# The memory's value projection as three float32r products, its norm's small products moved, in a fused decoder layer on one Trainium2 core

## The chip, the core and the metric

The kernel runs on one core of a Trainium2 chip. The core has a matrix engine (TensorE, PE in the profile, with its weight loads as PEld), three engines for elementwise work (VectorE or DVE, ScalarE or ACT, GpSimd or POOL), and SyncE (SP), from which this kernel issues all its DMA transfers. Each engine works through its own list of instructions in the order in which they were built and waits on semaphores for the others. The metric is the device time of one execution in microseconds (us). The median of three runs before the change is 1672.93 us (1672.88 to 1676.76).

## What is computed

One decoder layer over 1024 positions of width 1024. Its input is normalised by its root mean square, one combined projection gives the columns for stick-breaking attention, for an mLSTM and for the queries of a cross-attention into 256 memory tokens. The three branches are merged by gates, then a gated MLP follows. The change lies in what the memory needs:

```python
def _rmsnorm(x, g):
    xf = x.astype(jnp.float32)
    y = xf * lax.rsqrt(jnp.mean(xf * xf, axis=-1, keepdims=True) + EPS)
    return (y * g.astype(jnp.float32)).astype(x.dtype)

def _memory_cross_attention(q, mem_n, w_kv, g_q, g_k):
    k, v = jnp.split(mem_n @ w_kv, 2, axis=-1)
    qh = _rmsnorm(_split_heads(q, XA_HEADS), g_q)
    kh = _rmsnorm(_split_heads(k, XA_HEADS), g_k)
    vh = _split_heads(v, XA_HEADS)
    ...
h = _rmsnorm(x, g_mix[l])
... = jnp.split(h @ w_in[l], offsets, axis=-1)
y_xa = _memory_cross_attention(xa_q, _rmsnorm(mem, g_mem[l]), w_mem_kv[l], xa_g_q[l], xa_g_k[l])
```

The memory's norm is a factor per token, so the kernel projects `mem * g_mem` first and multiplies by the factor when it reads the sums.

## The kernel before

Everything is float32 in memory. A product is done in one of two ways. With float32 operands it is one call on PE, which the trace shows as two matmul records. With the type float32r, each operand is split into two tensors: hi, a rounded copy made by ACT, and lo, the rest, a subtraction on DVE (`split`, lines 135 to 137; `wsplit` allocates the pair). `mm3` (lines 148 to 151) then sums three products: hi by hi, hi by lo and lo by hi.

The start of the program is what the change touches, in the order in which it is written:

- `mem_load` (twice) loads half of the memory, transposed, into a tile of 128 x 1024 (tag `y`) and multiplies it by its gain on ACT (line 196) into a page `mg[j]`.
- `mem_w` loads one of four blocks of the weights for the keys (`w_kv[0]`) or the values (`w_kv[1]`). `mem_mm` multiplies a block with the memory, float32 by float32: four calls for each block (two halves of the tokens, two rows of 128 channels). The keys go to the banks `ps_z`, the values to `ps_pv`.
- `mem_stats` squares the memory (line 211), adds it up and has two small products with a column of ones (line 218), which give the sum per token.
- `x_page` loads the input in pieces of two channels blocks by 512 positions; `x_stats` squares them (line 274) and adds them on DVE (lines 277, 279); `rstd` takes four small products with ones (line 165) and a power on POOL (line 157); `spread` makes a diagonal of the result (line 177) and multiplies it with ones (line 179), so that the factor of each position stands in a row for all partitions. `x_norm` then multiplies the input by gain and factor (line 287) and splits it into `hh` and `hl` (the tiles `h`), and writes the unsplit form to DRAM (`hn_d`).
- After that follow the projections of the upper half of positions: queries and keys of the first head pair (`chunks`, banks `ps_pj`, two of them in turn), the gates (`gates_if`, line 462), then `nat_chunks` for the values. In between the lower half of the input is loaded (`xp[0]`) and normalised in the same way, and `mem_keys` and `mem_values` read the memory's sums.

A bank `ps_pj` is free again when ACT and DVE have read it: lines 374 to 377 for the queries, 381 to 386 for the keys.

The order on each engine is decided when the program is built: a scheduler goes through the calls above and places them by priority (`tc.high_priority` moves a part ahead by a number of places), and tiles with the same tag share a fixed number of buffers (`BUFS`): two each for `raw`, `whi`, `wlo`, five for `U`, sixteen for `pg`.

Of the kernel before, what the change touches and what calls it, by code (L numbers as in the profile page):

```python
# [18 lines left out]
P = 128  # L19
# [23 lines left out]
def tile_hybrid_layer(ctx: ExitStack, tc: tile.TileContext, xT, memT, vecs, w_t, w_n, w_kv, w_if,  # L43
# [143 lines left out]
    mraw = []  # L187
    mg = [page() for _ in range(2)]

    def mem_load(j):  # L190
        t = T([P, S], "y")
        mraw.append(t)
        nc.sync.dma_start(t.rearrange("p (k m) -> p k m", k=4), memT[4 * j:4 * j + 4].rearrange("k p m -> p k m"))
        for i in range(4):
            c = slice(i * NMEM, (i + 1) * NMEM)
            nc.scalar.activation(mg[j][:, c], t[:, c], AF.Copy, scale=col(C_GMEM + 4 * j + i))

    mtags = itertools.cycle(("raw", "whi", "wlo"))

    def mem_w(which, b):  # L200
        t = T([P, S], next(mtags))
        nc.sync.dma_start(t, w_kv[which, b])
# [5 lines left out]

    def mem_stats():
        for t in mraw:  # L210
            nc.scalar.activation(t, t, AF.Square)
        a = mraw[0]
        nc.vector.tensor_add(a, a, mraw[1])
        for n in (512, 256):
            nc.vector.tensor_add(a[:, :n], a[:, :n], a[:, n:2 * n])
        pc = bank("tr")
# [3 lines left out]

    def mem_mm(pm, w, b):
        for m in range(2):
            for kk in range(2):
                k = 2 * b + kk
                c = slice((k % 4) * NMEM + m * P, (k % 4) * NMEM + (m + 1) * P)
                nc.tensor.matmul(pm[m], mg[k // 4][:, c], w[:, hs(kk)], start=(k == 0), stop=(k == KT - 1))  # L226

    def mem_keys(pm, rm):
# [65 lines left out]
    mem_load(0)  # L294
    wk.append(mem_w(0, 0))
    mem_load(1)
    for b in range(1, 4):
        wk.append(mem_w(0, b))
        if b < 3:
# [6 lines left out]
    for g in range(2):  # L306
# [3 lines left out]
        nc.vector.tensor_sub(wif[:, :, 64 + 32 * g:68 + 32 * g], src, hi.bitcast(F32))  # L310
    mem_mm(pk, wk[0], 0)
    mem_mm(pk, wk[1], 1)
    rm = mem_stats()
    mem_mm(pk, wk[2], 2)
    mem_mm(pk, wk[3], 3)
    for b in range(4):
        wv.append(mem_w(1, b))
    r = rstd(x_stats(xp[1]), HALF)
    mem_mm(pv, wv[0], 0)
    x_norm(1, xp[1], spread(r, 4))  # L320
    for b in range(1, 4):
        mem_mm(pv, wv[b], b)

# [176 lines left out]
    for _ in range(3):  # L500
        next(vals)
    kn = mem_keys(pk, rm)
    mem_values(pv, rm)
# [906 lines left out]
```

## Time and profile before

| | before |
|---|---|
| median of three runs | 1672.93 us |
| the profiled execution | 1674.48 us |
| its span, first to last instruction | 1672.4 us |
| PE busy in the span | 1645.0 us (98%) |
| DVE busy | 1209.2 us (72%) |
| ACT busy | 826.8 us (49%) |
| POOL busy | 52.8 us (3%) |
| DMA, mean over the span | 127 GB/s |
| granted TensorE clock, mean | 1.000 |

The page of the profile gives such totals and the groups of instructions that cost most. For an edit in the first 60 us of 1672, the views that tell more are the timeline of each engine (start, length, engine, line, output from inputs, and in brackets how long the engine was idle before and who ended that), the list of waits, and the chain of work that ended last, here asked for a stretch of time. "x8" at the end of a timeline row says that eight instructions were merged into it.

### The profile page before, as it was taken

To read this page: it belongs to the slowest core of one execution; us is meant where nothing else is said; L and a number is where in the kernel's file an instruction comes from. 1 tells how busy PE (TensorE), PEld (TensorE's weight loads), DVE (VectorE), ACT (ScalarE), POOL (GpSimd) and SP (SyncE) were. 2 spreads that over 40 slices of the span, in tenths; PEclk is the share of its full clock that TensorE was granted. 3 is DMA by queue.
4 is the path that set the end of the run, shared out by engine and by line. 5 is a ranking of instruction groups with operands and counts; after the bars stand their busy time and mean duration, and the time that the engine had idled before them with its cause. 6 is when DMAs were issued, how large, how long until landed. Compare 5 with 4: busy or idle time off the path is not lost.

```text
span 1672.4 us, 21192 instructions
## 1 busy us (share of the span) xinstructions
PE 1645.0 (98%) x7975; PEld 1338.0 (80%) x7975; DVE 1209.2 (72%) x1710; ACT 826.8 (49%) x1249; POOL 52.8 (3%) x95
## 2 busy tenths in 40 slices
PE   8999999999999999999999999999999999999999
PEld 4777777788877888888788888688888888788887
DVE  5648778777765666666557648997778877789864
ACT  4547667645555445556422334565455554543431
POOL 1000000010000001000000000000000000000000
PEclk9999999999999999999999999999999999999999
DMA  8410011234324555433755354222222221486131
GB/s 296 149 64 24 35 39 51 95 116 137 108 104 154 183 183 170 133 127 113 271 181 184 114 189 145 94 90 104 78 77 76 82 87 58 164 327 239 36 138 73
DMA packets 96249, 212.69 MB, mean 127 GB/s; under 512 B 12416, under 2 KB 36224, under 8 KB 96148
## 3 DMA queue, kind: packets, MB, share of 16 engines
q1 hardware_dynamic: 96148, 211.35, 37.1%
q8 instruction: 63, 1.03, 0.3%
q14 instruction: 38, 0.31, 0.1%
HBM read 156.71 MB, written 54.61 MB: 126 GB/s over the span
## 4 chain that ended last, share of the span: by engine, by line
PE 89%; DVE 4%; ACT 4%; DMA 3%; issue 1%; SPq 0%; POOLq 0%; POOL 0%; ACTq 0%; DVEq 0%
PE ps_pj L149 14%; PE ps_pj L150 14%; PE ps_pj L151 14%; PE ps_pv L150 6%; PE ps_pv L151 6%; PE ps_pv L149 6%; PE ps_tr L151 4%; PE ps_tr L149 4%; PE ps_tr L150 4%; PE ps_z L149 3%; PE ps_z L150 3%; PE ps_z L151 3%; PE ps_tr L434 2%; PE ps_pv L448 1%; PE ps_z L226 1%; PE ps_z L413 1%
## 5 line engine op out<-in xcount | busy, mean ns | idle before, releaser
L150 PE MATMUL ps_pj<-h,whi 128*128 128x512 f32 x620 | 242.2, 391 | 0.0
L136 ACT ACTIVATE whi<-raw 128x512 fp32r<-128x512 f32 (+1 forms) x112 | 93.6, 836 | 177.5 <-PE ps_pj L150 71.6
L149 PE MATMUL ps_pj<-h,whi 128*128 128x512 f32 x412 | 163.2, 396 | 0.9 <-DVE U L1053 0.9
L149 PE MATMUL ps_pj<-pg,whi 128*128 128x512 f32 x396 | 154.6, 390 | 0.0
L151 PE MATMUL ps_pj<-pg,wlo 128*128 128x512 f32 x380 | 148.0, 389 | 0.0
L150 PEld LDWEIGHTS ps_pj<-h,whi 128*128 128x128 f32 x620 | 116.5, 188 | 23.5 <-issue 0.2
L151 PE MATMUL ps_pj<-h,wlo 128*128 128x512 f32 x332 | 129.9, 391 | 0.1
L810 DVE SCALAR_TENSOR_TENSOR y<-U,vec,y 128x1023 f32<-128x1023 f32 x88 | 112.5, 1280 | 8.0 <-ACT y L808 8.0
L422 DVE TENSOR_TENSOR_SCAN U<-U 128x512 f32<-128x512 f32 (+3 forms) x96 | 88.6, 965 | 30.7 <-ACT U L415 29.8
L149 PEld LDWEIGHTS ps_pj<-h,whi 128*128 128x128 f32 x412 | 77.4, 188 | 18.3 <-issue 1.5
L137 DVE TENSOR_TENSOR wlo<-raw,whi 128x1024 fp32r<-128x1024 f32 x54 | 66.0, 1222 | 30.9 <-ACT whi L136 30.6
L149 PEld LDWEIGHTS ps_pj<-pg,whi 128*128 128x128 f32 x396 | 74.3, 188 | 15.8 <-DVE pg L1051 0.4
L151 PEld LDWEIGHTS ps_pj<-pg,wlo 128*128 128x128 f32 x380 | 71.3, 188 | 14.9 <-issue 0.2
L136 ACT ACTIVATE whi<-pg 128x512 fp32r<-128x512 f32 (+1 forms) x59 | 43.4, 738 | 72.2 <-PE ps_pv L150 20.7
L150 PE MATMUL ps_pj<-pg,whi 128*128 128x512 f32 x188 | 73.4, 390 | 0.0
L151 PEld LDWEIGHTS ps_pj<-h,wlo 128*128 128x128 f32 x332 | 62.3, 188 | 13.6 <-DVE wlo L137 0.6
L150 PE MATMUL ps_pv<-h,whi 128*128 128x512 f32 x164 | 63.8, 389 | 0.0
L808 ACT ACTIVATE y<-U,vec 128x1024 f32<-128x1024 f32 x44 | 54.6, 1241 | 14.7 <-DVE U L712 14.6
L151 PE MATMUL ps_pj<-h,whi 128*128 128x512 f32 x156 | 60.8, 390 | 0.0
L137 DVE TENSOR_TENSOR wlo<-raw,wlo 128x512 fp32r<-128x512 f32 x58 | 39.9, 688 | 23.0 <-ACT wlo L136 22.7
L151 PE MATMUL ps_tr<-pg,wlo 128*128 128x512 f32 x144 | 56.2, 390 | 0.1
L137 DVE TENSOR_TENSOR whi<-raw,whi 128x512 fp32r<-128x512 f32 x58 | 39.9, 688 | 22.0 <-ACT whi L136 22.0
(438 smaller groups left out, 4306.0 us busy)
## 6 DMA issues: line engine op xcount, KB each, us to landing
raw<-in_w_t_dram SPq DMA_DIRECT2D x29, 512.0 KB
gate_d<-U SPq DMA_DIRECT2D x24, 512.0 KB
U<-gate_d SPq DMA_DIRECT2D x24, 512.0 KB
pg<-in_w_up_dram SPq DMA_DIRECT2D x22, 512.0 KB
act_d<-y SPq DMA_DIRECT2D x22, 512.0 KB
pg<-in_w_t_dram SPq DMA_DIRECT2D x21, 512.0 KB
raw<-in_w_dn_dram SPq DMA_DIRECT2D x18, 512.0 KB
raw<-in_w_o_dram SPq DMA_DIRECT2D x16, 512.0 KB
```

Of the source, the lines that this page charges most:

```text
L136: nc.scalar.activation(hi, src, AF.Copy)
L137: (eng or nc.vector).tensor_sub(lo, src, hi.bitcast(F32))
L149: nc.tensor.matmul(out, lh, rh, start=start, stop=False, skip_group_check=more)
L150: nc.tensor.matmul(out, lh, rl, start=False, stop=False, skip_group_check=more)
L151: nc.tensor.matmul(out, ll, rh, start=False, stop=stop, skip_group_check=more)
L226: nc.tensor.matmul(pm[m], mg[k // 4][:, c], w[:, hs(kk)], start=(k == 0), stop=(k == KT - 1))
L413: nc.tensor.matmul(z[:, a, :w], qs[a][:, ts(rb)], kz[a][:, c], start=False, stop=True)
L422: nc.vector.tensor_tensor_scan(f[:, a, 1:w + 1], f[:, a, 1:w + 1], f[:, a, 1:w + 1], 1.0 if o == 0 else f[:, a, 0:1], op0=ALU.mult, op1=AL ...
L434: nc.tensor.transpose(pt[:, a, ts(j)], g[:, a, ts(j)], ident)
L448: nc.tensor.matmul(pv[64 * a:64 * a + 64, ts(rb % 4)], sbv[s // 2][:, s % 2, (2 * p + a) * 64:(2 * p + a + 1) * 64], wt[:, a, ts(j)], star ...
L808: nc.scalar.activation(out, u, AF.Identity, bias=bias, scale=taps[0])
L810: nc.vector.scalar_tensor_tensor(out[:, :S - s], u[:, s:], taps[s], out[:, :S - s], op0=ALU.mult, op1=ALU.add)
```

## The change

The values are now computed with `mem_mm3`, that is with `mm3` on hi and lo of the memory (`mgr`, split in `mem_load`) and of each block of value weights. The keys stay as they are. The weights of the values are loaded into tiles `U`, `raw`, `raw`, `U` and split from there. The squares of the memory are added up by `mem_squares` into a tile `me` after all of this in the text of the program, and the two small products are called (`mem_rstd`) just before `mem_keys`. The small products of the input's norm (`rstd`) are called between the two halves of the last block of keys, and `spread` between the two halves of the first block of values.

```diff
--- before.py
+++ after.py
@@ -186,6 +186,7 @@
     nc.scalar.activation(warm, nhalf[:, :1], AF.Square)
     mraw = []
     mg = [page() for _ in range(2)]
+    mgr = [[page(dt=F32R) for _ in range(2)] for _ in range(2)]
 
     def mem_load(j):
         t = T([P, S], "y")
@@ -194,11 +195,10 @@
         for i in range(4):
             c = slice(i * NMEM, (i + 1) * NMEM)
             nc.scalar.activation(mg[j][:, c], t[:, c], AF.Copy, scale=col(C_GMEM + 4 * j + i))
-
-    mtags = itertools.cycle(("raw", "whi", "wlo"))
-
-    def mem_w(which, b):
-        t = T([P, S], next(mtags))
+        split(mg[j], *mgr[j])
+
+    def mem_w(which, b, tag):
+        t = T([P, S], tag)
         nc.sync.dma_start(t, w_kv[which, b])
         return t
 
@@ -206,24 +206,36 @@
     nc.vector.tensor_mul(gqk, col(C_GQ), col(C_GK))
     xkv_d = dtile([XAH, P, 2, NMEM], "xkv_d")
 
-    def mem_stats():
+    def mem_squares():
         for t in mraw:
             nc.scalar.activation(t, t, AF.Square)
-        a = mraw[0]
-        nc.vector.tensor_add(a, a, mraw[1])
-        for n in (512, 256):
-            nc.vector.tensor_add(a[:, :n], a[:, :n], a[:, n:2 * n])
+        a, b = mraw
+        out = T([P, HALF], "me")[:, :NMEM]
+        nc.vector.tensor_add(a, a, b)
+        nc.vector.tensor_add(a[:, :HALF], a[:, :HALF], a[:, HALF:])
+        nc.vector.tensor_add(out, a[:, :NMEM], a[:, NMEM:HALF])
+        return out
+
+    def mem_rstd(a):
         pc = bank("tr")
         for t in range(2):
             nc.tensor.matmul(pc[:, t:t + 1], a[:, ts(t)], ones[:, :1], start=True, stop=True)
         return rstd_cols(pc[:, :2], 2, D)
 
-    def mem_mm(pm, w, b):
-        for m in range(2):
+    def mem_mm(pm, w, b, ms=(0, 1)):
+        for m in ms:
             for kk in range(2):
                 k = 2 * b + kk
                 c = slice((k % 4) * NMEM + m * P, (k % 4) * NMEM + (m + 1) * P)
                 nc.tensor.matmul(pm[m], mg[k // 4][:, c], w[:, hs(kk)], start=(k == 0), stop=(k == KT - 1))
+
+    def mem_mm3(pm, w, b, ms=(0, 1)):
+        for m in ms:
+            for kk in range(2):
+                k = 2 * b + kk
+                c = slice((k % 4) * NMEM + m * P, (k % 4) * NMEM + (m + 1) * P)
+                mm3(pm[m], mgr[k // 4][0][:, c], mgr[k // 4][1][:, c], w[0][:, hs(kk)], w[1][:, hs(kk)],
+                    k == 0, k == KT - 1)
 
     def mem_keys(pm, rm):
         kns = []
@@ -292,10 +304,10 @@
     xp = {0: [], 1: []}
     wk, wv = [], []
     mem_load(0)
-    wk.append(mem_w(0, 0))
+    wk.append(mem_w(0, 0, "raw"))
     mem_load(1)
     for b in range(1, 4):
-        wk.append(mem_w(0, b))
+        wk.append(mem_w(0, b, ("raw", "whi", "wlo")[b - 1]))
         if b < 3:
             xp[1] += [x_page(1, i) for i in (2 * b - 2, 2 * b - 1)]
     wraw = T([P, KT, 8], "hf")
@@ -308,18 +320,26 @@
         hi = wif[:, :, 32 * g:32 * g + 4]
         nc.scalar.activation(hi, src, AF.Copy)
         nc.vector.tensor_sub(wif[:, :, 64 + 32 * g:68 + 32 * g], src, hi.bitcast(F32))
-    mem_mm(pk, wk[0], 0)
-    mem_mm(pk, wk[1], 1)
-    rm = mem_stats()
-    mem_mm(pk, wk[2], 2)
-    mem_mm(pk, wk[3], 3)
-    for b in range(4):
-        wv.append(mem_w(1, b))
-    r = rstd(x_stats(xp[1]), HALF)
-    mem_mm(pv, wv[0], 0)
-    x_norm(1, xp[1], spread(r, 4))
-    for b in range(1, 4):
-        mem_mm(pv, wv[b], b)
+    for b in range(3):
+        mem_mm(pk, wk[b], b)
+    wraws = [mem_w(1, 0, "U")]
+    a = x_stats(xp[1])
+    wraws += [mem_w(1, b, ("raw", "raw", "U")[b - 1]) for b in range(1, 4)]
+    mem_mm(pk, wk[3], 3, (0,))
+    r = rstd(a, HALF)
+    mem_mm(pk, wk[3], 3, (1,))
+    wv.append(wsplit(None, raw=wraws[0]))
+    mem_mm3(pv, wv[0], 0, (0,))
+    rows = spread(r, 4)
+    wv.append(wsplit(None, raw=wraws[1]))
+    x_norm(1, xp[1], rows)
+    mem_mm3(pv, wv[0], 0, (1,))
+    mem_mm3(pv, wv[1], 1)
+    for b in range(2, 4):
+        with tc.high_priority(offset=200):
+            wv.append(wsplit(None, raw=wraws[b]))
+        mem_mm3(pv, wv[b], b)
+    squares = mem_squares()
 
     def proj(src, rh, rl, consume, halves=(1, 0), tag="pj"):
         wh, wl = wsplit(src)
@@ -499,6 +519,7 @@
     x_norm(0, xp[0], spread(r, 4))
     for _ in range(3):
         next(vals)
+    rm = mem_rstd(squares)
     kn = mem_keys(pk, rm)
     mem_values(pv, rm)
     for _ in range(4):
```

With the scheduler, this moves instructions on all engines up to the normalisation of the lower half of x; behind that the order of every engine is what it was. Three places matter below. Lines of the changed program are numbered 12 to 21 higher than before. In these rows a tile has its buffer's running number, and names ahead of `<-` are written.

DVE, from the normalisation of the upper half of x to the split of the first projection's weights. Line 287 makes a half page of the normalised x, the next row on an `h` is its lo. `wlo_74` and `wlo_78` are the lo of the weights for queries and keys, `pg_64` that of the first weights for the values of the attention. Before (the row behind the last one shown is `wlo_78`):

```order
L137 TENSOR_TENSOR wlo_74_303<-raw_72_300,whi_73_302 128x1024
L137 TENSOR_TENSOR h_16_111<-U_53_232,h_8_103 128x512
L287 SCALAR_TENSOR_TENSOR U_54_240<-pg_32_143,vec_92,ps_tr_51_222 128x512
L137 TENSOR_TENSOR h_17_112<-U_53_232,h_9_104 128x512
L287 SCALAR_TENSOR_TENSOR U_54_240<-pg_32_143,vec_92,ps_tr_51_222 128x512
L137 TENSOR_TENSOR h_18_113<-U_54_240,h_10_105 128x512
L287 SCALAR_TENSOR_TENSOR U_55_248<-pg_33_145,vec_92,ps_tr_51_222 128x512
L137 TENSOR_TENSOR h_19_114<-U_54_240,h_11_106 128x512
L287 SCALAR_TENSOR_TENSOR U_55_248<-pg_33_145,vec_92,ps_tr_51_222 128x512
L137 TENSOR_TENSOR h_20_115<-U_55_248,h_12_107 128x512
L137 TENSOR_TENSOR pg_64_283<-y_62_280,pg_63_282 128x1024
L137 TENSOR_TENSOR h_21_116<-U_55_248,h_13_108 128x512
```

In the changed program `wlo_84` and `wlo_88` belong to queries and keys. The lo of the last two blocks of the memory's value weights, `wlo_62` and `wlo_64`, stand seven and three rows ahead of the first one shown:

```order
L137 TENSOR_TENSOR h_20_115<-U_58_238,h_12_107 128x512
L299 SCALAR_TENSOR_TENSOR U_59_246<-pg_36_151,vec_92,ps_tr_49_199 128x512
L137 TENSOR_TENSOR h_21_116<-U_58_238,h_13_108 128x512
L299 SCALAR_TENSOR_TENSOR U_59_246<-pg_36_151,vec_92,ps_tr_49_199 128x512
L137 TENSOR_TENSOR h_22_117<-U_59_246,h_14_109 128x512
L299 SCALAR_TENSOR_TENSOR U_60_254<-pg_37_153,vec_92,ps_tr_49_199 128x512
L137 TENSOR_TENSOR h_23_118<-U_59_246,h_15_110 128x512
L299 SCALAR_TENSOR_TENSOR U_60_254<-pg_37_153,vec_92,ps_tr_49_199 128x512
L137 TENSOR_TENSOR h_24_119<-U_60_254,h_16_111 128x512
L137 TENSOR_TENSOR wlo_84_353<-raw_82_350,whi_83_352 128x1024
L137 TENSOR_TENSOR h_25_120<-U_60_254,h_17_112 128x512
L137 TENSOR_TENSOR wlo_88_388<-raw_86_385,whi_87_387 128x1024
```

The lo of the weights for the queries has moved from the first third of these rows to their end, with that for the keys two rows behind it, and two splits of the memory's weights stand ahead.

SP, at the loads of the lower half of x (`in_xT_dram`), before:

```order
L142 DMA raw_76_335<-in_w_t_dram 128x1024
L142 DMA raw_85_399<-in_w_n_dram 128x1024
L289 DMA hn_d_117<-U_54_240 128x1024
L289 DMA hn_d_117<-U_55_248 128x1024
L266 DMA pg_68_292<-in_xT_dram 128x2x512
L266 DMA pg_69_294<-in_xT_dram 128x2x512
```

and in the changed program:

```order
L301 DMA hn_d_121<-U_59_246 128x1024
L301 DMA hn_d_121<-U_60_254 128x1024
L142 DMA raw_95_449<-in_w_n_dram 128x1024
L142 DMA raw_98_455<-in_w_n_dram 128x1024
L278 DMA pg_78_342<-in_xT_dram 128x2x512
L278 DMA pg_79_344<-in_xT_dram 128x2x512
```

Two loads of weights now stand ahead of those of x. `raw_98` takes the buffer of `raw_86`, which is free once `wlo_88` has been computed on DVE.

ACT, between the square of the first loaded page of x (`pg_68` before, `pg_78` now) and the last read of the bank of the first keys, before:

```order
L274 ACTIVATE U_93_438<-pg_68_292 128x1024
L374 ACTIVATE pg_56_272<-ps_pj_75_306 64x512
L375 ACTIVATE pg_57_273<-ps_pj_75_306 64x512
L274 ACTIVATE U_94_440<-pg_69_294 128x1024
L274 ACTIVATE U_95_443<-pg_70_296 128x1024
L381 ACTIVATE pg_58_274<-ps_pj_79_341 64x512
L382 ACTIVATE pg_59_275<-ps_pj_79_341 64x512
L383 ACTIVATE pg_58_274<-ps_pj_79_341 64x512
L384 ACTIVATE pg_59_275<-ps_pj_79_341 64x512
```

and in the changed program:

```order
L286 ACTIVATE U_103_488<-pg_78_342 128x1024
L136 ACTIVATE whi_96_451<-raw_95_449 128x1024
L394 ACTIVATE pg_66_322<-ps_pj_85_356 64x512
L395 ACTIVATE pg_67_323<-ps_pj_85_356 64x512
L286 ACTIVATE U_104_490<-pg_79_344 128x1024
L286 ACTIVATE U_105_493<-pg_80_346 128x1024
L286 ACTIVATE U_106_496<-pg_81_348 128x1024
L136 ACTIVATE whi_99_457<-raw_98_455 128x1024
L401 ACTIVATE pg_68_324<-ps_pj_89_391 64x512
L402 ACTIVATE pg_69_325<-ps_pj_89_391 64x512
L403 ACTIVATE pg_68_324<-ps_pj_89_391 64x512
L404 ACTIVATE pg_69_325<-ps_pj_89_391 64x512
```

Two copies of weights and one square have come between the page's arrival and the last read of that bank.

## The prediction

> **What bounds the kernel now.** I read the page's totals first, then PE's waits, then the chain of waits in the stretch that the change touches.
>
> ```profile
> span 1672.4 us, 21192 instructions
> PE 1645.0 (98%) x7975; PEld 1338.0 (80%) x7975; DVE 1209.2 (72%) x1710; ACT 826.8 (49%) x1249; POOL 52.8 (3%) x95
> ```
>
> PE is busy for 98% of the span, so time that is taken from PE or added ahead of it tends to reach the end. The list of PE's waits up to 140 us (engine, line, whom it waited for: total, times, longest) has these at its start:
>
> ```profile
> PE ps_z L226 <- ACT pg L196: 6.9, 1, 6.9
> ...
> PE ps_pj L462 <- DVE pg L377: 0.6, 1, 0.6
> ...
> PE ps_pj L149 <- DVE pg L386: 0.5, 1, 0.5
> ```
>
> After its first product at 6.9 us PE waits only twice in the first 60 us, 1.1 us together, both times for a bank that DVE has yet to read (lines 377 and 386). The chain behind the second wait (start, length, what) shows who set it:
>
> ```profile
> 28.22 2.06 DVE U L287 x3
> ...
> 38.35 0.33 SPq L289
> ...
> 38.73 0.44 SPq L266
> ...
> 40.03 8.37 DMA pg<-in_xT_dram
> ...
> 53.58 0.70 DVE pg L386
> ...
> 54.42 0.47 PE ps_pj L149
> ```
>
> From 28.22 us, when the row factor of the upper half of x is ready, DVE works through the normalisation; SP can issue the loads of the lower half of x (line 266) only behind the last `hn_d` store; ACT squares those pages before it reads the banks; and PE gets its bank at 54.42. PE's full work hides this chain up to 0.5 us. So the question is not only what PE saves, but whether this chain grows.
>
> **What PE saves.** Rows of PE's timeline (start, length, line, output from inputs):
>
> ```profile
> 31.45 3.60 PE L226 MATMUL ps_pv<-raw,pg 128*128 128x512 f32 x8
> 34.89 3.60 PE L226 MATMUL ps_pv<-whi,pg 128*128 128x512 f32 x8
> ...
> 45.62 0.39 PE L151 MATMUL ps_pj<-h,wlo 128*128 128x512 f32 x1
> ...
> 49.02 0.39 PE L151 MATMUL ps_pj<-h,wlo 128*128 128x512 f32 x1
> 49.96 0.45 PE L462 MATMUL ps_pj<-h,pg 128*100 128x512 f32 x1 [0.55 <-DVE pg L377]
> ...
> 53.50 0.40 PE L463 MATMUL ps_pj<-h,pg 128*100 128x512 f32 x1
> ...
> 62.71 0.94 PE L165 MATMUL ps_tr<-ones,U 128*128 128x1 f32 x8
> 63.51 0.49 PE L149 MATMUL ps_pj<-whi,h 128*128 128x512 f32 x1
> ```
>
> A block of value weights takes 34.89 - 31.45 = 3.44 us, four blocks 13.76. The 15 float32r products from 45.62 to 49.02 take 0.227 each; the 48 that replace the four blocks take 10.9. PE saves **2.9 us**. The two small products of the memory's norm move into the stream of float32r products. There eight records of such products took 63.51 - 62.71 = 0.8 us; theirs are four, **0.4 us**, and they come after the stretch below, where nothing takes them in. Where they stood, among the keys, PE now is done earlier but then waits, so I count no gain for it.
>
> **What ACT and DVE get.** The splits are new work for them: six copies and six subtractions of 128x1024. Rows of both, of POOL and PE:
>
> ```profile
> 5.56 1.70 ACT L196 ACTIVATE pg<-y,vec 128x256 f32<-128x256 f32 x4 [3.33 <-DMA y<-in_memT_dram]
> ...
> 10.13 1.06 ACT L211 ACTIVATE y<-y 128x1024 f32<-128x1024 f32 x1
> ...
> 18.46 0.35 ACT L309 ACTIVATE pg<-hf 128x32 fp32r<-128x32 f32 x2 [0.47 <-DMA hf<-in_w_if_dram]
> ...
> 46.24 1.06 ACT L274 ACTIVATE U<-pg 128x1024 f32<-128x1024 f32 x1 [1.36 <-DMA pg<-in_xT_dram]
> ...
> 48.42 2.01 ACT L274 ACTIVATE U<-pg 128x1024 f32<-128x1024 f32 x2
> ```
>
> ```profile
> 11.22 1.23 DVE L213 TENSOR_TENSOR y<-y,y 128x1024 f32<-128x1024 f32 x1 [7.31 <-ACT y L211]
> 12.48 1.15 DVE L215 TENSOR_TENSOR y<-y 128x512 f32<-128x512 f32 x2
> 13.79 0.91 DVE L305 MEMSET pg<- 128x1024 f32 x1 [0.16 <-issue]
> ...
> 19.29 0.69 DVE L279 TENSOR_TENSOR U<-U 128x512 f32<-128x512 f32 x1
> ...
> 25.11 0.88 DVE L177 TENSOR_SCALAR hf<-ident,sm 128x128 f32<-128x128 f32 x4 [1.13 <-POOL sm L157]
> ...
> 40.74 1.22 DVE L137 TENSOR_TENSOR wlo<-raw,whi 128x1024 fp32r<-128x1024 f32 x1
> ```
>
> ```profile
> 16.78 1.70 POOL L157 TENSOR_TENSOR sm<-sm,nhalf 128x2 f32<-128x2 f32 x1 [13.11 <-DVE sm L155]
> 24.07 1.01 POOL L157 TENSOR_TENSOR sm<-sm,nhalf 128x4 f32<-128x4 f32 x1 [5.59 <-DVE sm L155]
> ...
> 27.16 1.02 PE L179 MATMUL ps_tr<-hf,ones 128*128 128x512 f32 x2
> ```
>
> I follow the new order with these lengths up to the row factor of x.
>
> - On ACT each half of the memory now takes gain, copy and square: 5.56 + 2 x (1.70 + 1.06 + 1.06) = 13.2 us, against 11.2 before.
> - DVE then adds the memory's squares and clears the gate-weight page, in this order: 13.2 + 1.23 + 1.15 + 0.91 = 16.5, with the gaps 16.6. The two copies of line 309 wait for that page, and now stand ahead of the squares of x on ACT: 17.0, then four squares at 1.0 (48.42: two in 2.01): 21.0.
> - DVE: three sums from 19.0 on, 22.7; lo of the first value block 23.9; last sum 24.6; lo of the second block 25.8.
> - PE has then finished the keys (6.9 + 1.7 us of slow start, shown below, + 4 x 3.44 = 22.4) and waits for that first lo. Its small products end at 25.4, the scaling on DVE at 26.0. The power on POOL costs 1.01 or 1.70 us: the first of the program took 1.70, and this one is now the first, so 27.7. Diagonals 28.6; the product by line 179 and its way to DVE took 28.22 - 27.16 = 1.1 plus its weight load: **29.9**, against 28.22.
>
> From there to the end of `wlo_78` (40.74 + 1.22 = 41.96) DVE needed 13.74 us before, for eight rows of line 287, eight lo of h and three of 128x1024. The changed order has as many of each up to `wlo_88` (its three are `wlo_64`, `wlo_84`, `wlo_88`), and must wait some 0.4 us for the copy of the fourth block, whose buffer PE frees late: 29.9 + 13.74 + 0.4 = **44.0 us**. The loads of x now stand on SP behind `raw_98`, which waits for `wlo_88`: first x load at 44.4, against 38.73. What is queued on SP behind it, the weights of the next projection, has slack.
>
> How long the load takes is not settled by the trace. The first page of the memory, with little ahead, is the row below; before, the first x page took 46.24 - 38.73 = 7.5 us, behind two stores.
>
> ```profile
> 1.18 4.29 DMA y<-in_memT_dram
> ```
>
> I take 5.0, nearer to the first, since only loads stand right ahead: 49.4 (48.7 to 51.9). Of the stretches of the start, this one (length, busy time of each engine, clock, DMA share, GB/s) has the transfers nearly back to back:
>
> ```profile
> 12.00:23.00 11.00, 11.00 (x32) 5.17 (x30) 7.11 (x11) 4.58 (x6) 1.70 (x1) 1.00 0.94 368
> ```
>
> [...]
>
> Behind the page, ACT and DVE needed 53.58 + 0.70 - 46.24 = 8.04 us before to the end of the second bank's read. Now one more square and two copies of weights stand between: + 3 x 1.02 = 11.1. PE starts its first product of the attention's values at 49.4 + 11.1 + 0.1 = **60.6** instead of 54.42: +6.2. The saving of 2.9 us is inside this number, since PE arrives early and waits. With the 0.4: **+6.6 us**.
>
> After that, the order of all engines is as before, and each later wait of PE hangs on work that starts from PE's own products, so I take the shift to the end. The mem keys now follow the normalisation of the lower half, and PE has banks of 24 products (5.4 us each) to fill meanwhile; their transposes should not wait.
>
> The profiled execution took 1674.48 us (span 1672.4), 1.55 above the median; 1674.48 + 6.6 = 1681.1 for such an execution, **1679.5** for the median of 1672.93.
>
> **The rivals.** A measurement of this kernel can tell about 0.3% (5.0 us) from no change.
>
> *PE's own path decides (not slower).* If the x pages land before 47.8, the banks come early, and what is left is the wait for `wlo_84`: 44.0 - 1.22 - 0.61 = 42.2; the 44 products left of two banks, 10.0 us, and sixteen of line 462 and 463 at (53.50 - 49.96)/15 = 0.236, 3.8, give 56.0: +1.6, with the 0.4 +2.0, 1674.9. It holds up to +5.0, and needs a load in under 3.4 us; for it speaks that loads may run undisturbed by stores, against it the rows of 4.29 and 7.5. Chance 0.2.
>
> *The saving stays.* If DVE's front part is not on the path, PE keeps 2.9 - 0.4 and perhaps the 1.1 of waits: 1669.5, still within 0.3%. Against it: 5.8 us would have to be missing from DVE's sum. Chance 0.02.
>
> *The pages land as late as before.* 7.5 us after issue: 51.9 + 11.2 = 63.1, +8.7 + 0.4: 1682.0. For it: two loads stand just ahead in the queue, and 7.5 and 8.37 are the only values for these pages at this place. Chance 0.2, with a tail beyond.
>
> *A later wait takes part of it in*, one that does not move with PE: PE's waits after 60 us would have to shrink by 2 us or more; 1675 to 1677.5. Chance 0.06.
>
> *PE's tempo falls in its new pause.* At the start, after 6.9 us of rest, weight loads of line 226 followed each other at twice the later distance:
>
> ```profile
> 8.75 0.33 PEld L226 LDWEIGHTS ps_z<-raw,pg 128*128 128x128 f32 x1 [0.52 <-issue]
> 9.60 0.33 PEld L226 LDWEIGHTS ps_z<-raw,pg 128*128 128x128 f32 x1 [0.52 <-issue]
> 10.37 0.19 PEld L226 LDWEIGHTS ps_z<-raw,pg 128*128 128x128 f32 x1 [0.44 <-issue]
> 10.80 0.19 PEld L226 LDWEIGHTS ps_z<-raw,pg 128*128 128x128 f32 x1 [0.24 <-issue]
> ```
>
> 0.85 against 0.43 us, four times: 1.7 us. The longest of PE's waits after that, in the list for the whole span, is no longer than this:
>
> ```profile
> PE ps_pv L149 <- ACT pg L136: 1.7, 1, 1.7
> ```
>
> If the pause before `wlo_84` (from about 38.6 to 42.2, 3.6 us) did the same, PE would be 1.7 us later at the next bank, for which it then waits 4 us anyway: no change to the forecast, and 1676.6 instead of 1674.9 in the first rival. [...]
>
> **How the numbers follow.** Forecast (+5 to +8 us) 0.52; landing late 0.2; PE's own path 0.2; partly taken in 0.06; saving kept 0.02. Slower by over 0.3%: 0.52 + 0.2 + a third of the 0.06 = 0.74; within: 0.25; faster 0.01. The range leaves out half of the first rival and the tail of late landings: 1675.4 to 1683.0. Its ends are those of the load (4.29 and 7.5 us) widened by about 1 us for the sum on DVE and below to the middle of the first rival.
>
> **What would show it.** Right: on SP the first x load near 44.4; ACT's first square of the lower half at 48.7 to 52; PE waits of 3 to 4 us for a lo by line 137 at the queries' bank and of 3 to 5 us for the subtraction that is line 386 now; `ps_pv` products 0.23 apart. Wrong: the row factor's first use well before 29 us, the x load before 42, no wait of PE above 2 us behind 30 us, or a shift that shrinks behind 60 us.

## The result, and the profile after

The changed kernel takes **1682.97 us** (median of 6 runs, 1681.26 to 1684.04), the kernel before 1673.57 us on the same chip (6 runs, 1672.88 to 1676.76). The ratio is **1.0052, 95% interval 1.0041 to 1.0062**: slower by half a per cent. The profiled execution of the changed kernel took 1681.26 us, the fastest of its six. Its page:

```profile
span 1679.5 us, 21243 instructions
PE 1646.5 (98%) x7991; PEld 1343.3 (80%) x7991; DVE 1217.9 (73%) x1716; ACT 831.6 (50%) x1255; POOL 52.2 (3%) x95
```

The span is 7.1 us longer. PE's busy time is no shorter although 2.9 us of work were taken out; the reason is for the most part the clock, below. The list of PE's waits up to 140 us (engine, tile, line, whom it waited for: total, times, longest) now has, of what is new:

```profile
PE ps_z L230 <- ACT pg L197: 6.4, 1, 6.4
PE ps_pj L151 <- DVE wlo L137: 3.1, 1, 3.1
PE ps_pj L482 <- DVE pg L397: 2.3, 1, 2.3
...
PE ps_pj L149 <- DVE pg L406: 0.8, 1, 0.8
```

The chain that the prediction follows, in rows of the timeline (start, length, engine, line, output from inputs, in brackets the idle time ahead and who ended it):

```profile
25.63 1.03 POOL L157 TENSOR_TENSOR sm<-sm,nhalf 128x4 f32<-128x4 f32 x1 [21.97 <-DVE sm L155]
...
29.27 2.06 DVE L299 SCALAR_TENSOR_TENSOR U<-pg,vec,ps_tr 128x512 f32<-128x512 f32 x3
...
41.80 1.23 DVE L137 TENSOR_TENSOR wlo<-raw,whi 128x1024 fp32r<-128x1024 f32 x1
...
43.48 2.08 SPq L278 DMA_DIRECT2D pg<-in_xT_dram  x4
...
50.67 1.06 ACT L286 ACTIVATE U<-pg 128x1024 f32<-128x1024 f32 x1 [9.52 <-DMA pg<-in_xT_dram]
...
60.95 0.69 DVE L406 TENSOR_TENSOR pg<-ps_pj,pg 64x512 fp32r<-64x512 f32 x1
...
61.79 0.47 PE L149 MATMUL ps_pj<-pg,h 128*128 128x512 f32 x1 [0.84 <-DVE pg L406]
```

The row factor is first used at 29.27, `wlo_88` ends at 43.03, the first x load is issued at 43.48, the page is there 7.2 us later, and PE starts the first product of the attention's values at 61.79 instead of 54.42: 7.4 us late, and the span ends 7.1 late. What was not foreseen as a part of it stands in the windows of the same profile (stretch, length, busy time of PE, PEld, DVE, ACT and POOL, granted clock of PE, DMA share, GB/s):

```profile
40.00:45.00 5.00, 3.66 (x10) 2.92 (x11) 5.00 (x6) 1.16 (x2) 0.00 (x0) 0.69 0.65 233
45.00:50.00 5.00, 5.00 (x23) 4.10 (x22) 0.29 (x1) 0.00 (x0) 0.00 (x0) 0.97 0.90 310
55.00:60.00 5.00, 4.49 (x13) 3.16 (x14) 4.87 (x5) 4.94 (x7) 0.00 (x0) 0.66 0.28 102
```

Behind each of the two long waits PE runs at half clock: the clock is at 0.50 from 41.9 to 45.3 and from 55.6 to 59.0, 3.4 us each (a window at half clock, below). In those stretches the float32r products follow each other at 0.43 us instead of 0.227. Before, no window of this stretch was below 1.00. The mean clock of a run counts such windows: two of 3.4 us at half lose 3.4 us of 1679.5, so 0.998, which is what this run has. The other five runs of the changed kernel have 0.996 to 0.998, three of them 0.997, which is three windows; their spans are 1680.5 to 1682.2. Where the windows of these runs lie was not profiled.

### The profile page after: what moved, and what is told of

It reads as the page before. It is cut to its first block, busy times and chain, and to the rows that moved or that the text cites. A ratio compares the mean times of both kernels' runs of the same rounds, so it can differ in the third digit from the quotient of the medians.

```text
span 1679.5 us, 21243 instructions
## 1 busy us (share of the span) xinstructions
PE 1646.5 (98%) x7991; PEld 1343.3 (80%) x7991; DVE 1217.9 (73%) x1716; ACT 831.6 (50%) x1255; POOL 52.2 (3%) x95
## 3 DMA queue, kind: packets, MB, share of 16 engines
q8 instruction: 63, 1.03, 0.3%
## 4 chain that ended last, share of the span: by engine, by line
PE 89%; DVE 4%; ACT 4%; DMA 2%; issue 1%; SPq 0%; POOLq 0%; POOL 0%; DVEq 0%; ACTq 0%
PE ps_pj L149 14%; PE ps_pj L150 14%; PE ps_pj L151 14%; PE ps_pv L150 6%; PE ps_pv L151 6%; PE ps_pv L149 6%; PE ps_tr L149 4%; PE ps_tr L151 4%; PE ps_tr L150 4%; PE ps_z L149 3%; PE ps_z L151 3%; PE ps_z L150 3%; PE ps_tr L454 1%; PE ps_pv L468 1%; PE ps_z L433 1%
## 5 line engine op out<-in xcount | busy, mean ns | idle before, releaser
L136 ACT ACTIVATE whi<-pg 128x512 fp32r<-128x512 f32 (+1 forms) x59 | 43.5, 738 | 71.4 <-PE ps_pv L150 20.2
L151 PEld LDWEIGHTS ps_pj<-h,wlo 128*128 128x128 f32 x332 | 62.8, 189 | 17.2 <-DVE wlo L137 4.1
```

The lines of the kernel that those rows point to most:

```text
L136: nc.scalar.activation(hi, src, AF.Copy)
L151: nc.tensor.matmul(out, ll, rh, start=False, stop=stop, skip_group_check=more)
```

## The experiments

Two theories stood against each other at first. **Late chain**: the loss is the chain above, and the x loads are its pivot. **Waits for lo alone**: PE is late by its waits for the lo of weights, and the loads cost nothing. From the first results on a third had to be weighed, **half clock**: a pause of PE costs more than it lasts. All runs in one table; "bank" is the start of PE's first product of the attention's values in the profiled execution, where the kernel shows one that waits. e1 to e4, e5 to e8 and e9 to e12 ran on three different chips, so kernels of different groups are compared by the ratio to the kernel before on the same chip.

| kernel | span | bank | ratio to before (95%) | mean clock of its runs |
|---|---|---|---|---|
| before | 1672.4 | 54.42 | 1 | 0.999 to 1.000, 4 of 67 lower |
| changed | 1679.5 | 61.79 | 1.0052 (1.0041 to 1.0062) | 0.996 to 0.998 |
| e1 x early | 1676.7 | 59.10 | 1.0044 (1.0031 to 1.0058) | 0.997, once 0.999 |
| e2 values f32 | 1678.3 | 58.90 | 1.0023 (1.0014 to 1.0032) | 0.997 to 1.000 |
| e3 norm back | 1683.8 | 63.13 | 1.0063 (1.0050 to 1.0075) | 0.997 to 0.999 |
| e4 e1, POOL clears | 1675.3 | 59.22 | 1.0031 (1.0020 to 1.0041) | 0.997 to 0.999 |
| e5 e4, POOL subtracts | 1675.3 | | 1.0021 (1.0012 to 1.0030) | 0.998 to 1.000 |
| e6 e1, pause filled | 1675.0 | 59.15 | 1.0019 (1.0010 to 1.0028) | 0.999 to 1.000 |
| e7 e2, old buffers | 1673.5 | 54.54 | 0.9993 (0.9984 to 1.0002) | 0.998 to 1.000 |
| e8 e5, norm in a wait | 1675.5 | | 1.0010 (1.0000 to 1.0019) | 0.998 to 1.000 |
| e9 raw buffers | 1683.9 | 61.52 | 1.0069 (1.0056 to 1.0082) | 0.996, once 0.997 |
| e10 queries first | 1671.0 | 52.91 | 1.0002 (0.9992 to 1.0011) | 0.999 to 1.000 |
| e11 pause filled | 1675.6 | 57.95 | 1.0025 (1.0014 to 1.0036) | 0.998 to 1.000 |
| e12 filled less | 1677.8 | 58.27 | 1.0033 (1.0020 to 1.0046) | 0.997 to 0.999 |

**e1: the x loads written early.**

```diff
+    xp[0] = [x_page(0, i) for i in range(4)]
     st, chunks = sb_qk(0)
...
-    xp[0] = [x_page(0, i) for i in range(4)]
     for _ in chunks((1,)):
```

> The changed kernel, with the loads of the lower half of x written ahead of the weights of the queries: on SP they now stand ahead of the loads that wait for the lo of the queries' and keys' weights. Theory (late chain: lo's on DVE, x loads on SP, pages, squares, bank reads): the loads are issued before 35 us, ACT's squares of the lower half no longer wait for a page, the two waits of PE behind 45 us (2.3 us at line 482 and 0.8 at 149 in the changed kernel) fall below 1 us in total, the wait of 3 us for the queries' lo stays; about 3 us come back of the loss: span about 1676.5, ratio to the kernel before 1.0025 to 1.0035. Rival A (PE is late by its waits for the lo alone, and the late pages cost nothing of their own): ratio stays at 1.005. Rival B (transfers are the limit: the early x pages delay the value weights): PE waits longer for the value weights' split than 1.7 us, ratio 1.005 or more.

The loads are issued at 20.2 to 32.4 us; the wait at line 482 is gone and that at 149 is 0.5 us. PE's waits and one row of ACT:

```profile
PE ps_pj L151 <- DVE wlo L137: 3.1, 1, 3.1
...
PE ps_pj L149 <- DVE pg L406: 0.5, 1, 0.5
```

```profile
54.04 1.06 ACT L136 ACTIVATE whi<-raw 128x1024 fp32r<-128x1024 f32 x1 [2.84 <-PE ps_pj L150]
```

The profiled execution does what the late chain says (span 1676.7, 2.8 us of the 7.1 come back), and speaks against the first rival. The median does not: 1.0044 against the expected 1.0025 to 1.0035, and the rival's 1.005 lies within its interval. The profiled run is the one of five with a mean clock of 0.999; the four with 0.997 have spans of 1679.1 to 1681.0. The ACT row shows a way for a slow PE to reach the chain: the copy of the next weights waits for the buffer that PE still reads, and the reads of the keys' bank stand behind that copy.

**e2 and e7: the values as before, with the new and with the old buffers.** In e2 the first part of the change is undone:

```diff
-        split(mg[j], *mgr[j])
...
-    wv.append(wsplit(None, raw=wraws[0]))
-    mem_mm3(pv, wv[0], 0, (0,))
+    mem_mm(pv, wraws[0], 0, (0,))
```

and so for the other blocks. e7 differs from e2 in the buffers of the value weights alone:

```diff
-    wraws = [mem_w(1, 0, "U")]
+    wraws = [mem_w(1, 0, "raw")]
...
-    wraws += [mem_w(1, b, ("raw", "raw", "U")[b - 1]) for b in range(1, 4)]
+    wraws += [mem_w(1, b, ("whi", "wlo", "raw")[b - 1]) for b in range(1, 4)]
```

> The changed kernel without its first part: the values of the memory again as 16 f32 products, without the splits of memory and value weights; the places of the small products, of the spread and the loads stay as changed. Theory (the work of the splits on ACT and DVE makes the chain late, the moved small products cost 0.4 us): x loads issued at 39 to 40.5 us, no wait of PE above 1.5 us between 10 and 60 us, span +1 to +2 us on the kernel before, ratio 1.0005 to 1.0012. Rival A (the moved small products and spread are what costs): ratio at 1.004 or above. Rival B (something behind 60 us, such as the mem keys late, costs most): the shift grows behind 62 us by over 2 us.

> As e2 (values as f32 products, moved small products and spread), but the value weights are loaded into the buffers of the kernel before (raw, whi, wlo, raw) instead of U, raw, raw, U. Theory: the moves themselves cost nothing but 0.4 us; what made e2 slower are the U buffers that the weights take from the squares of x, which put squares behind the gate weights' copies and the x loads behind 40 us. So: row factor used by 28.3 us, x loads issued before 38.5 us, no wait of PE above 1 us between 10 and 60 us, ratio 0.9993 to 1.0007. Rival (the moves cost it): ratio as e2's, 1.0017 to 1.003.

e2 came close in the loads (40.84 us) and the longest wait (1.6 us), but the ratio is 1.0023 (the profiled span is 5.9 us longer; this execution is the slowest of the eleven): the late chain as stated does not explain it. The bank is 4.5 us late, and a fall to half clock from 60.1 to 63.5, behind that wait, adds some 1.2 us: behind 100 us PE is 5.7 us late. Rows of ACT, and the first rows of x on DVE:

```profile
14.77 1.06 ACT L284 ACTIVATE U<-pg 128x1024 f32<-128x1024 f32 x1 [0.28 <-DMA pg<-in_xT_dram]
18.98 0.35 ACT L319 ACTIVATE pg<-hf 128x32 fp32r<-128x32 f32 x2 [3.15 <-DMA hf<-in_w_if_dram]
19.23 1.99 ACT L284 ACTIVATE U<-pg 128x1024 f32<-128x1024 f32 x2
```

```profile
29.27 2.06 DVE L297 SCALAR_TENSOR_TENSOR U<-pg,vec,ps_tr 128x512 f32<-128x512 f32 x3 [1.22 <-PE ps_tr L179]
```

The same rows of e7:

```profile
15.79 1.06 ACT L284 ACTIVATE U<-pg 128x1024 f32<-128x1024 f32 x1 [0.30 <-DMA pg<-in_xT_dram]
17.14 1.06 ACT L284 ACTIVATE U<-pg 128x1024 f32<-128x1024 f32 x1 [0.29 <-DMA pg<-in_xT_dram]
18.65 0.35 ACT L319 ACTIVATE pg<-hf 128x32 fp32r<-128x32 f32 x2 [0.45 <-DMA hf<-in_w_if_dram]
```

```profile
26.78 2.06 DVE L297 SCALAR_TENSOR_TENSOR U<-pg,vec,ps_tr 128x512 f32<-128x512 f32 x3 [2.15 <-PE ps_tr L179]
```

In e2 the copies of the gate weights stand ahead of two squares of x and wait 3.2 us for their data; in e7 they stand behind all four. The row factor follows: 29.27 against 26.78. So the moved small products and the spread cost nothing that can be seen (e7: 0.9993, loads at 36.09), and with f32 values 0.0030, the whole distance between e2 and e7, hangs on where the value weights are loaded. The rows show another order on ACT; that it comes from there being two U buffers fewer for the squares is read from the edit.

**e3: the memory's norm back among the keys**, with the values as three products:

```diff
-    for b in range(3):
-        mem_mm(pk, wk[b], b)
+    mem_mm(pk, wk[0], 0)
+    mem_mm(pk, wk[1], 1)
+    rm = mem_rstd(mem_squares())
+    mem_mm(pk, wk[2], 2)
```

> The changed kernel with the norm of the memory back at its old place: its two small products and its power stand among the keys, behind the second block of key weights; values as three float32r products. Theory: PE spends 0.4 us less at line 222 behind 60 us and the row factor of x comes 0 to 0.6 us later, so that the ratio is that of the changed kernel within 0.0006: 1.0045 to 1.0055. Rival A (the moved norm delays the mem keys, and these the later part): ratio 1.003 or less.

1.0063, more than either said; its interval overlaps that of the changed kernel. Moving the norm late at least did not cost the 7 us. Its profile shows two stretches at half clock again, from 42.4 and from 62.8, and a third from 1059.5, of which more in the last section.

**e4: as e1, and POOL clears the page of the gate weights.**

```diff
-    nc.vector.memset(wif.bitcast(F32), 0.0)
+    nc.gpsimd.memset(wif.bitcast(F32), 0.0)
```

> As e1, and the page of the gate weights is cleared by POOL instead of DVE, which takes 0.9 us out of DVE's front part. Theory (DVE's sum before the row factor of x is on the path): PE's wait for the first lo of the value weights goes from 1.5 to below 0.8 us, the row factor is used about 1.2 us earlier than in e1, and the span is 1.0 to 1.5 us below e1's. Rival A (ACT's copies and squares, not DVE, set the row factor): the span of e1 within 0.4 us. Rival B (POOL's clearing takes longer than 2 us and holds the copies of the gate weights up): later than e1.

The first `hn_d` store is issued at 30.23 instead of 31.56, the medians are 2.1 us apart (1678.90 against 1681.01), the spans 1.4. That DVE's part before the row factor is on the path is not shown by this: the intervals of the two ratios overlap, and the bank comes no earlier, 59.22 against 59.10; in this execution the clock stood at 0.50 for two windows, 40.4 to 47.2. At 340 us PE is 4.2 us late in both profiles; the 1.4 us come later.

**e5 and e8: POOL subtracts for the first queries' and keys' lo.** e5 passes another engine to the split; e8 also computes the memory's norm ahead of the spread.

```diff
-    for _ in chunks((1,)):
+    for _ in chunks((1,), nc.gpsimd):
```

```diff
+    squares = mem_squares()
+    rm = mem_rstd(squares)
     rows = spread(r, 4)
```

> As e4, and POOL instead of DVE subtracts for the lo of the first queries' and keys' weights, so that PE need not wait 3 us for them. In the profiles so far the granted clock stood at 0.50 for 3.4 to 6.8 us behind PE's pauses, and the mean clock of most runs with such a pause was 0.997, against 0.999 to 1.000 for the kernel before. Theory (late chain, and PE at half clock behind a pause): no wait of PE above 1.2 us between 10 and 60 us, no stretch at 0.50 there, the mean clock 0.999 or 1.000 in nearly all runs, ratio 0.9985 to 1.0003. Rival A (the clock costs nothing, since later waits take it in): e4's ratio less the 3.1 and 0.7 us of waits, 1.0008, with mean clocks as in e4. Rival B (POOL needs over 3 us for one subtraction, or holds DVE up): a wait of over 1.5 us for the lo stays, ratio 1.0015 or more.

> As e5, and the two small products of the memory's norm stand ahead of the spread of x's row factor, where PE waits 0.9 to 1.1 us for DVE and POOL anyway, instead of behind 60 us. Theory: the 2.9 us that the float32r values save reach the end for the most part: PE waits for 1 us or less in total between 10 and 60 us, 2 to 3 us faster than the kernel before, ratio 0.9980 to 0.9990. Rival A (the 0.4 us are lost again, since POOL's two powers follow each other): as e5. Rival B (POOL's subtraction comes late): a wait of over 1.5 us for the lo, ratio 1.0005 or more.

Both missed. e5, POOL and DVE:

```profile
34.69 5.33 POOL L137 TENSOR_TENSOR wlo<-raw,whi 128x1024 fp32r<-128x1024 f32 x2 [7.41 <-ACT whi L136]
```

```profile
34.27 0.68 DVE L137 TENSOR_TENSOR h<-U,h 128x512 fp32r<-128x512 f32 x1
...
35.53 2.22 DVE L137 TENSOR_TENSOR h<-U,h 128x512 fp32r<-128x512 f32 x1
37.67 0.73 DVE L299 SCALAR_TENSOR_TENSOR U<-pg,vec,ps_tr 128x512 f32<-128x512 f32 x1
38.33 2.24 DVE L137 TENSOR_TENSOR h<-U,h 128x512 fp32r<-128x512 f32 x1
```

POOL takes 2.67 us for one subtraction, DVE 1.22. And DVE's own subtraction takes 2.2 us instead of 0.68 while POOL works, so rival B is right in that DVE is held up: twice 1.5 us. The row of line 299 between the two, which reads the bank `ps_tr`, takes 0.73 us beside POOL, and 0.74 at 33.61, before POOL starts. Why the one kind of row got longer and the other did not was not shown. The wait for the lo fell from 3.1 to 0.7 us, but 1.2 us at line 482 and 0.9 us for rows of h took its place. Up to 60 us e5's profile has no fall to half clock; e8's has one, from 51.5 to 54.9, behind the 1.2 us.

**e6: as e1, with PE kept busy in the pause.**

```diff
-lambda *a: itertools.chain(proj_chunks(w_t[T_SBQ + p], eq, *a),
+lambda *a, fill=0: itertools.chain(proj_chunks(w_t[T_SBQ + p], eq, *a, fill=fill),
...
+            for _ in range(fill):
+                nc.tensor.matmul(p, wh[:, ts(0)], hh[0][:, hs(h)], start=True, stop=True)
             for k in range(KT):
...
-    for _ in chunks((1,)):
+    for _ in chunks((1,), fill=16):
```

> As e1, but PE is kept busy in its pause: ahead of the products of the first queries' and the first keys' bank stand 16 products each of the same operands, which the first real product overwrites. Nothing of the output changes, and DVE, ACT and SP have the same work. Theory (a pause costs more than its length, since PE runs at half clock behind it): no stretch at 0.50 between 38 and 48 us, the mean clock 0.001 to 0.002 higher than e1's 0.997, and a ratio of 1.0020 to 1.0034 although the 16 products shift some of DVE's work. Rival (the clock is a reading only, or is taken in by later waits): ratio 1.004 to 1.005.

The text on record speaks of both banks; the edit fills that of the queries alone, 16 products (8007 on PE against 7991). Windows of e6, where e1 has 0.71 and 0.95:

```profile
40.00:45.00 5.00, 4.62 (x21) 3.48 (x20) 5.00 (x7) 5.00 (x8) 0.00 (x0) 1.00 0.96 352
45.00:50.00 5.00, 3.88 (x17) 2.92 (x16) 4.96 (x6) 3.26 (x5) 0.00 (x0) 1.00 0.14 48
```

PE does 16 products more, all for nothing, and the kernel is **faster**: 1.0019 against 1.0044, intervals apart (medians of 1677.31 and 1681.01 us). All its 11 runs have a mean clock of 0.999 or 1.000, and four of e1's five have 0.997, so some two windows fewer. That the clock is the cause is likely but not shown. Rows of DVE, ACT and SP also changed places. And in the profiled executions the bank comes at the same time (59.15 and 59.10) and PE is equally late at 340 us (4.0 and 4.2); e6's shorter span comes from behind that, where the clock is at 1.00 in e1 throughout and in e6 but for one window near 1050 us. The runs of e1 with 0.997 are not profiled, so where their windows lie is not known.

**e9: only the buffers of the changed kernel**, raw for all four value blocks (the diff as in e7, with "raw" throughout).

> The changed kernel with one edit: the four blocks of value weights are loaded into raw buffers only, instead of U, raw, raw, U, so that the squares and rows of x have the U buffers for themselves. Theory (part of the loss is that the weights take U buffers, as e2 against e7 showed for f32 values): the squares of x are not held up on ACT, the row factor is used at 27 to 28.3 us (29.27 in the changed kernel), the x loads start 1.5 to 2.5 us earlier than its 43.48, the pause for the queries' lo stays at 2.5 us or more with half clock behind it, and the ratio falls from 1.0052 to 1.0025 to 1.0042. Rival (with float32r values the splits on DVE set the row factor, and the buffers don't matter): 1.0046 or more.

The row factor came earlier, as expected, but the x loads only by 0.6 us (42.87), and this is the slowest of all, 1.0069. DVE, ACT and windows of e9:

```profile
27.60 2.06 DVE L299 SCALAR_TENSOR_TENSOR U<-pg,vec,ps_tr 128x512 f32<-128x512 f32 x3
```

```profile
50.31 1.06 ACT L136 ACTIVATE whi<-raw 128x1024 fp32r<-128x1024 f32 x1 [8.97 <-PE ps_pj L150]
```

```profile
40.00:45.00 5.00, 2.52 (x6) 2.04 (x7) 5.00 (x7) 0.63 (x1) 0.00 (x0) 0.65 0.57 213
45.00:50.00 5.00, 5.00 (x16) 3.94 (x16) 0.30 (x1) 0.00 (x0) 0.00 (x0) 0.67 0.89 298
```

The rows show a loop: PE pauses, then runs at half clock for two windows (41.4 to 48.3); so it gives the buffer of the queries' weights back late; ACT's copy waits for that until 50.31, and the squares of x and the bank reads stand behind the copy; PE waits again, and the clock falls again (61.9 to 65.3). What the loop costs is not separated: the first square starts at 51.28 against 50.67 in the changed kernel, but the bank comes at 61.52 against 61.79, and most of the 4.4 us between the two spans arise behind it. An earlier row factor was worth nothing here; why this kernel is the slowest stays open.

**e10: the lo of the queries first.** As e4, with the split of the first queries' weights and the bank's reads at a higher priority, the first clearings on POOL at the program's start, and the norm ahead of the spread.

```diff
-        with tc.high_priority(offset=SOON):
+        with tc.high_priority(offset=soon):
             wh, wl = wsplit(src)
...
-    for _ in chunks((1,)):
+    for _ in chunks((1,), 200):
...
+    kz0 = [kz_pages()]
     wif = T([P, KT, P], "pg", F32R)
```

> As e4 (x loads early, gate page cleared by POOL), with three more edits and all subtractions on DVE: the split of the first queries' weights has so high a priority that DVE does it between the rows of x, ahead of the last of them; POOL clears the halves of the first keys' pages at the start of the program, where DVE has nothing to do; the two small products of the memory's norm stand ahead of the spread. Theory: PE waits for no lo longer than 0.8 us, the diagonals on DVE take 0.9 us instead of the 2.2 us that they took beside POOL's clearing, no stretch at half clock, mean clock 0.999 to 1.000, and PE keeps half to one us of its 2.9: ratio 0.9988 to 1.0000. Rival (the rows of x, now later, hold PE up as much as the lo did): waits for h of over 2 us, ratio 1.0015 or more.

PE's waits and its row at the bank:

```profile
PE ps_pj L149 <- DVE pg L413: 1.1, 1, 1.1
...
PE ps_pj L150 <- DVE h L137: 0.3, 1, 0.3
...
PE ps_pj L151 <- DVE wlo L137: 0.2, 1, 0.2
```

```profile
52.91 0.47 PE L149 MATMUL ps_pj<-pg,h 128*128 128x512 f32 x1 [1.05 <-DVE pg L413]
```

No long pause and no half clock in the first 60 us, the bank 1.5 us earlier than before (of which 0.6 is an earlier first product of PE, 6.30 against 6.91), span 1671.0. The loss of the changed kernel is gone, 1.0002, and the interval spans 1: of PE's saving nothing is to be seen in the time, and no version here beats the kernel before. Five edits were made at once, so which of them did it is not separated.

**e11 and e12: the changed kernel with 16 and with 6 filling products**, again for the queries' bank alone; between the two the order on ACT, POOL and SP is the same, and on DVE but for one row.

> The changed kernel with PE kept busy in its pause before the queries' lo: 16 products each of the same operands ahead of the real ones of the first queries' and the first keys' bank, which the first real product overwrites. The order on DVE, ACT and SP moves a little by it, the x loads come 1 to 2 us earlier; e12 has the same order with fewer products. Theory (half clock behind the pause): no stretch at 0.50 behind the queries' lo (one may stand behind the later pause near 58 us), mean clock higher than e12's by 0.001 or more, ratio 1.0022 to 1.0038, and lower than e12's by 0.0008 to 0.0025. Rival: the two alike within 0.0005.

> As e11, with 6 products each instead of 16; DVE, ACT and SP have the same instructions in the same order, only PE's pause before the queries' lo is longer by 2.3 us. Theory: one or two windows at half clock behind it, mean clock 0.997 to 0.998, ratio 1.0036 to 1.0052. Rival (a pause costs only what it lasts, and here nothing, since the lo comes when it comes): as e11 within 0.0005.

1.0025 and 1.0033 are not told apart, and the mean clocks hardly differ; this pair does not show that filling pays. Both ratios lie below the changed kernel's, e12's with overlapping intervals; the edit also brought the x loads forward, to 41.84 and 42.10. e12's profile has both pauses and no slow window up to 60 us:

```profile
PE ps_pj L151 <- DVE wlo L137: 2.8, 1, 2.8
PE ps_pj L149 <- DVE pg L408: 2.7, 1, 2.7
```

```profile
40.00:45.00 5.00, 3.34 (x15) 2.77 (x16) 5.00 (x6) 1.48 (x2) 0.00 (x0) 1.00 0.73 232
55.00:60.00 5.00, 2.29 (x11) 1.57 (x10) 4.85 (x7) 2.70 (x5) 0.00 (x0) 1.00 0.33 108
```

e11's profile, with 0.5 and 2.6 us, has a fall from 58.3 to 61.7. So a pause of 2.6 to 2.8 us brought half clock in one run and not in another.

## Why the prediction came out as it did

The sign and the chain hold, and the sum holds for the profiled execution: +7.1 us of span against +6.6. The medians lie 9.4 us apart, because the profiled execution of the kernel before was 0.9 us slower than its median and that of the changed kernel 1.7 us faster. The median of 1682.97 against the forecast 1679.5 is inside the range by 0.03 us, and that is luck: two terms, the landing and the clock, were too small. Step by step:

- **PE's saving** is as worked out (`ps_pv` products 0.227 apart), and it is inside a wait, as said. e10 shows what is left of it without the long waits: 0.9 us at the bank.
- **Row factor, 29.9**: 29.27. The power on POOL took 1.03, not the 1.70 of "the first of the program". The size was nearly right, but not the cause that its heading gives, the new work of the splits, alone: e9 has the same splits and 27.60, earlier than before. The 1.7 us between them hang on the buffers, and so on the one step in the list that is not about splits, the gate weights' copies ahead of the squares of x on ACT. In the changed kernel they wait 3.7 us for the page that DVE clears. That e2, without splits, has the same 29.27 is a coincidence: there the copies wait for their data, and until 18.98.
- **DVE's sum of 13.74** from there to the end of `wlo_88`: 43.03 - 29.27 = 13.76. The extra 0.4 did not come. First x load 43.48, foreseen 44.4.
- **Landing, 5.0 us: the term that was mis-sized.** It took 7.2. The rival in which the pages land as late as before (7.5 us, 1682.0) had this term right, and comes nearer to the median than the forecast. Two weight blocks, 1.0 MB, had been issued just ahead, from 41.37 on, and the queue moved 233 to 310 GB/s there, not 368. What made the landing late was not tested by itself.
- **ACT's and DVE's chain, 11.1**: 61.64 - 50.67 = 10.97.
- **PE's waits**: 3.1 for the lo, as said. At line 406 (before: 386) 0.8 instead of 3 to 5: PE had waited 2.3 at line 482 and then done that line's products at half clock.
- **The clock, which the prediction has as PE's tempo and priced at "no change to the forecast"**: in the profiled execution that is nearly so, since both windows end in waits that stand anyway. It need not be so in the other runs: the profiled execution was the fastest, with two windows, and the typical run has three by its mean clock. A window behind which no wait takes it in costs 0.9 to 1.3 us (last section). The third may be one near 1050 us, which kernels without the splits have too, so it is not shown that it belongs to the change. How much of the changed kernel's own median is due to the clock e11 and e12 do not settle.
- **The 0.4 us for the norm at the later place**: e3 undid it and gained nothing; e8, which put it into a wait, and e5 differ by 1.3 us in the median, with overlapping intervals.
- **The way to the end**: PE is 7.4 us late at the bank, 8.2 at 140 us and 7.1 at the end, so what lies between took in about 1 us. No later wait of 2 us went away.

Of the loss of 0.52%, then: the moves cost nothing (e7); with f32 values the order on ACT that came with the U buffers costs 0.30% (e2 against e7); the splits add 0.29% (the changed kernel against e2). That they do so by holding up the queries' lo, the x loads and, through PE's pauses, the clock is read from the profiles. The parts do not simply add: with the splits there, other buffers made it worse (e9).

## What to carry to other kernels

Work taken from a full PE pays only if the engines that feed it have room for what the saving needs: here six copies and six subtractions at the start, where DVE sets the pace, together with other buffers for the loads, turned 2.9 us of saving into some 9 us of loss. When a change opens a pause of 2 to 3 us on PE, price the pause with the time at half clock that may follow it (here 3.4 us at 0.50, which cost 0.9 to 1.3 us where no wait took it in), and look who waits for PE's buffers during it. A new buffer for a load can reorder another engine: look at the order on each engine before the cause is given to the new work.

## What the runs showed of the hardware

- **Half clock after short, incomplete pauses.** In the first 70 us the clock fell to 0.50 for 3.4 us, or twice that, at waits of 1.2 to 3.1 us: from 1.0 us ahead of the end of the wait (e9, 41.4) to 1.2 us behind it (e2, 60.1). In the 3.4 us ahead of each of eleven such falls PE was still busy for 0.6 to 2.2 us. Not every such wait had a fall: in e12 waits of 2.8 and 2.7 us had none, in e5 one of 1.2 us had none. What decides it was not shown.
- **The same wait with and without a fall, and its price.** Near 1050 us PE waits 1.7 us for ACT in all fourteen profiles (the wait that the prediction names as the longest behind the first one), with the same instructions behind. In eight of them (e3, e5 to e8, e10 to e12) the clock falls to 0.50 for 3.4 us, in six it does not, the kernels before and changed among these. The mean clocks agree: e5, e6, e7, e10 and e12 have 0.999 with no fall from 20 to 70 us, the kernel before has 1.000. From this wait to a later product, here e7 with a fall and the kernel before without one:

```profile
1047.43 0.50 PE L149 MATMUL ps_pv<-pg,whi 128*128 128x512 f32 x1 [1.72 <-ACT pg L136]
...
1058.58 0.50 PE L149 MATMUL ps_pj<-h,wlo 128*128 128x512 f32 x1
```

```profile
1047.81 0.50 PE L149 MATMUL ps_pv<-pg,whi 128*128 128x512 f32 x1 [1.72 <-ACT pg L136]
...
1057.68 0.50 PE L149 MATMUL ps_pj<-h,wlo 128*128 128x512 f32 x1
```

The six profiles without a fall take 9.87 us for this, the eight with one 10.75 to 11.18: 0.9 to 1.3 us for one window. The runs of the kernel before agree on average: the 38 with a mean clock of 0.999 are 1.0 us longer than the 25 with 1.000 (by chip 1.5, 1.1 and -0.2, the last with four runs at 1.000).

- **DVE slower beside POOL, not only beside subtractions.** In e1 two clearings on POOL fell onto the four diagonals on DVE: 2.16 us instead of 0.88 in the changed kernel, where POOL is idle then. In e5 the diagonals take 2.16 us beside clearings from 25.29 to 27.28; in e4 and e6 PE waits 1.1 us for them, as in e1 and e5.

```profile
26.75 2.16 DVE L177 TENSOR_SCALAR hf<-ident,sm 128x128 f32<-128x128 f32 x4 [1.14 <-POOL sm L157]
26.78 0.95 POOL L389 MEMSET pg<- 64x1024 f32 x1
27.78 0.98 POOL L390 MEMSET pg<- 64x1024 f32 x1
```

- **Useless products may pay.** With 16 products of 0.227 us in a pause e6 has a ratio 0.0025 below e1's, some 4 us, and no mean clock below 0.999. The edit also moved work on other engines, and e11 against e12 shows no such gain, so that the filling did it is not shown.
